# Decay differences in one operation per level, exponentials that carry signs and the key factor, and a new order in attention and gates

## The chip, the core and the metric

One core of a Trainium2 chip runs the whole program. The time is device microseconds of one execution. The kernel before takes 1636.86 us (median of three runs, 1635.97 to 1637.5).

## What is computed

Two transformer blocks over 512 tokens of width 1024, in fp32. The change lies in two mixers. One is the attention of block 1 (8 query heads, 2 groups of keys), whose keys are also compressed to one per 16 tokens:

```python
hp = rmsnorm(x, norm1_g) @ w_in                 # q, and keys and values of three branches
kc = rmsnorm(gelu(blocks(k0 + pe_k) @ wk1) @ wk2)   # compressed keys
vc = gelu(blocks(v0 + pe_v) @ wv1) @ wv2            # compressed values
q, k1, k2 = rmsnorm(q), rmsnorm(k1), rmsnorm(k2)    # per head of 64
o = g0*softmax(q kc^T) vc + g1*softmax(q k1^T, chosen blocks) v1 + g2*softmax(q k2^T, window) v2
```

The other is the gated recurrence of block 2 (4 heads of 128, two directions, the state first run over 256 context tokens):

```python
lf = logaddexp(log(lb), log1p(-lb) + log_sigmoid(z))   # log decay
k  = (1 - lb) * sigmoid(-z)
b  = cumsum(lf)
a[t, s] = sum_k q[t, k] * exp(b[t, k] - b[s, k]) * k[s, k]   # s <= t
o  = a @ v + (q * exp(b)) @ S
```

## The kernel before

**Products.** A product in fp32 is done as three matmuls on split halves (high and low part), by the helper `mm3` (L210 to L212). Weights come in by a DMA on SyncE's queue (`wload`, L222; two raw buffers), ScalarE makes the high part `wh` (L188 is its helper `act`), VectorE or GpSimd the low part `wl` (L191 is the helper `tt`; three buffers). PSUM has four banks for products ("mm"), one ("sm") and three ("aux").

**Who sets the order.** A scheduler puts the instructions of each engine into an order. It goes by the order in which the code emits them, and by priorities: weight loads are drawn ahead by `self.ahead` places. Every engine then works strictly through its own row, so an instruction that waits holds up all behind it.

**The gated recurrence** (`hgrn`, `hg_head`). `pj(h)` projects head h's gates: zf and zb (forward and backward; 512 tokens and 256 of context each) and the query q. `sig` turns them into `hgk` (key, one tile per direction), `hgkc` (key of the context) and `hgq`. Then `hg_head(h)` is emitted, and after it `pj(h+1)`, whose products are what TensorE has to do while a head's chain runs on the other engines. In `hg_head` ScalarE takes logarithms, giving log decays (`hgl`, and `hglc` for the context); VectorE scales the keys by 1−lb (`omlb`) and sums the logs by scans (L1450, L1452). The context's key goes through an exponential, a multiplication into `hgkc` and two transposes on TensorE (L1459) to the first state `hgS`. For the 512 tokens the matrix `a` is built in levels: blocks of 128 are cut in halves of 64, 32, 16 and 8. At each level `hgE` holds b minus a reference row for the later half, and the reference minus b for the earlier half: two subtractions of half width, the one on GpSimd, the other on VectorE. One exponential covers the four levels (128x2048). Later halves are multiplied by q, earlier ones by k. `hgek` and `hgeq` are the same for the innermost blocks. TensorE multiplies (L1515 for the innermost, L1525 and L1537 for the levels); `hgA` collects the results: a masked product, three plain copies per direction on VectorE (L1531) and eight copies under a mask (L1540). `hgke` and `hgqe` carry the state from block to block; its transposes come back through ScalarE as `hgkt`, and L1549, L1553 and L1554 form state and output.

**The attention** (`nsa_proj`). Eight projections of 128 columns in the order of the list `order`: the compressed branch's key and value (4, 5) first, then the keys 6 and 7, then q (0 to 3). Behind each of the six q and k tiles, squares are summed per head by a matmul (L859) into one bank with 12 rows. The compression (`compress`: 64 small matmuls, L971, a GELU, transposes, two small products, a norm with a power on GpSimd, `kcbd` and `vcz`) is a generator that is advanced once behind each projection but the first two. Behind the projections come the product for V (128x280), the start of the next product (ysH, `merge`), the norm factors broadcast by L879 (the tile `rb`), and `stack`, which splits q and k into halves (`qs`, `ks`) on ScalarE, VectorE and, for two of the q tiles, GpSimd. Then come the scores (L1061, L1063), the scores against compressed keys (L1019), and the transposes of the probabilities (L1083).

## Time and profile before

| | |
|---|---|
| median of three runs | 1636.86 us |
| the profiled execution | 1638.55 us |
| its span in the trace | 1636.8 us |
| mean granted clock of TensorE | 0.979 |
| TensorE busy | 1567.7 us, 96% |
| VectorE busy | 1130.2 us, 69% |
| ScalarE busy | 746.1 us, 46% |
| GpSimd busy | 418.0 us, 26% |

The times of rows and windows are counted from the start of the span. A granted clock of 1.00 in a window is the level of 2.4 GHz, 0.50 that of 1.2 GHz; values between are mixtures. "Idle before" is the time that an engine stood still ahead of an instruction, and the releaser is what ended it.

### The profile page before, as it was taken

The numbers are of one execution on the slowest core, as the hardware profiler recorded it, in microseconds if no ns is written. First come the engines' busy times: TensorE is split into PE (matmuls) and PEld (weight loads), VectorE is DVE, ScalarE is ACT, GpSimd is POOL, SyncE is SP. The second block draws the span as 40 slices with busy tenths as digits, with TensorE's granted clock in tenths as the row PEclk, the third lists the DMA queues.
The fourth block names the chain that finished last, engine by engine and source line by source line (L and its number), as shares of the span: only waits on it lengthen the run. The fifth ranks groups of instructions, "written<-read, shape, count | busy, mean of one in ns | idle before, by whom it ended". The sixth has DMA issues, their size and how long they took to land.

```text
span 1636.8 us, 22811 instructions
## 1 busy us (share of the span) xinstructions
PE 1567.7 (96%) x8573; PEld 1302.8 (80%) x8573; DVE 1130.2 (69%) x2141; ACT 746.1 (46%) x1301; POOL 418.0 (26%) x377
## 2 busy tenths in 40 slices
PE   7799998999999999999999999989989999999997
PEld 5678876677898888888887888878879888888886
DVE  8886626776679744763528788576877798676745
ACT  4364427553444213352335555556554664333432
POOL 1010204213000000000112222315320697555553
PEclk9899997999999999999999999999999999999999
DMA  5222510003356753832211011111211232323222
GB/s 179 75 81 64 158 47 26 20 21 117 104 192 217 243 198 130 262 109 90 84 64 65 27 39 52 60 52 52 65 65 57 91 103 91 103 90 103 91 87 81
DMA packets 58734, 157.85 MB, mean 96 GB/s; under 512 B 11904, under 2 KB 18816, under 8 KB 58496
## 3 DMA queue, kind: packets, MB, share of 16 engines
q1 hardware_dynamic: 58624, 156.40, 29.4%
q8 instruction: 67, 1.10, 0.3%
q14 instruction: 43, 0.35, 0.1%
HBM read 152.57 MB, written 2.10 MB: 94 GB/s over the span
## 4 chain that ended last, share of the span: by engine, by line
PE 79%; DVE 13%; ACT 5%; issue 2%; POOL 1%; DMA 0%; SPq 0%; DVEq 0%; ACTq 0%
PE ps_mm L210 22%; PE ps_mm L211 22%; PE ps_mm L212 22%; PE ps_sm L1094 2%; DVE wl L191 2%; PE ps_mm L1083 1%; DVE caccm L200 1%; ACT L188 1%; DVE hgE L191 1%; PE ps_sm L761 1%; ACT wh L188 1%; PE ps_aux L1537 1%; DVE caccf L200 1%; PE ps_mm L971 0%; PE ps_aux L1061 0%
## 5 line engine op out<-in xcount | busy, mean ns | idle before, releaser
L188 ACT ACTIVATE wh<-raw 128x1024 fp32r<-128x1024 f32 (+3 forms) x234 | 236.8, 1013 | 514.0 <-PE ps_mm L211 406.5
L191 DVE TENSOR_TENSOR wl<-raw,wh 128x1024 fp32r<-128x1024 f32 (+2 forms) x162 | 198.2, 1224 | 114.9 <-ACT wh L188 107.9
L200 DVE SCALAR_TENSOR_TENSOR caccf<-ps_mm,cwf,caccf 128x441 f32<-128x441 f32 (+2 forms) x278 | 188.5, 695 | 30.9 <-ACT ctapf L188 24.7
L191 POOL TENSOR_TENSOR wl<-raw,wh 128x1024 fp32r<-128x1024 f32 (+2 forms) x72 | 160.2, 2225 | 166.8 <-ACT wh L188 166.8
L212 PE MATMUL ps_mm<-h4H,wl 128*128 128x512 f32 (+1 forms) x352 | 131.2, 375 | 0.0
L211 PE MATMUL ps_mm<-h4L,wh 128*128 128x512 f32 (+1 forms) x352 | 131.1, 375 | 0.0
L210 PE MATMUL ps_mm<-h4H,wh 128*128 128x512 f32 (+1 forms) x352 | 129.7, 377 | 0.6 <-DVE caccf L200 0.4
L191 POOL TENSOR_TENSOR rr<-rv,nhalf 128x2 f32<-128x2 f32 x9 | 8.6, 957 | 431.9 <-DVE rv L197 431.9
L210 PE MATMUL ps_mm<-h2H,wh 128*128 128x512 f32 (+1 forms) x280 | 103.8, 372 | 0.0
L212 PE MATMUL ps_mm<-h2H,wl 128*128 128x512 f32 (+1 forms) x280 | 103.6, 371 | 0.0
L211 PE MATMUL ps_mm<-h2L,wh 128*128 128x512 f32 (+1 forms) x280 | 103.6, 371 | 0.0
L210 PE MATMUL ps_mm<-aH,wh 128*128 128x512 f32 (+1 forms) x272 | 102.6, 377 | 0.5 <-DVE x L191 0.5
L212 PE MATMUL ps_mm<-aH,wl 128*128 128x512 f32 (+1 forms) x272 | 102.7, 378 | 0.0
L211 PE MATMUL ps_mm<-aL,wh 128*128 128x512 f32 (+1 forms) x272 | 102.4, 377 | 0.0
L210 PE MATMUL ps_mm<-hH,wh 128*128 128x512 f32 x224 | 89.5, 406 | 10.0 <-ACT hH L188 9.0
L1229 DVE CUSTOM_DVE_ANT_0 msc<-wmod,cB,cols 128x1024 bf16<-128x1024 f32 x64 | 81.9, 1280 | 21.0 <-DMA wmod<-in_wmod 20.8
L211 PE MATMUL ps_mm<-hL,wh 128*128 128x512 f32 x224 | 89.7, 401 | 0.0
L212 PE MATMUL ps_mm<-hH,wl 128*128 128x512 f32 x224 | 89.5, 400 | 0.0
L211 PEld LDWEIGHTS ps_mm<-h4L,wh 128*128 128x128 f32 x352 | 66.2, 188 | 12.3 <-DVE h4L L200 0.4
L212 PEld LDWEIGHTS ps_mm<-h4H,wl 128*128 128x128 f32 x352 | 66.2, 188 | 12.2
L210 PEld LDWEIGHTS ps_mm<-h4H,wh 128*128 128x128 f32 x352 | 65.0, 188 | 13.5 <-issue 0.8
L210 PE MATMUL ps_mm<-faH,wh 128*128 128x512 f32 (+1 forms) x194 | 72.3, 373 | 0.0
(544 smaller groups left out, 4081.3 us busy)
## 6 DMA issues: line engine op xcount, KB each, us to landing
raw<-in_wup SPq DMA_DIRECT2D x76, 512.0 KB, 3.5
wmod<-in_wmod SPq DMA_DIRECT2D x48, 512.0 KB, 4.4
raw<-in_wdn SPq DMA_DIRECT2D x32, 512.0 KB, 3.5
raw<-in_win SPq DMA_DIRECT2D x28, 512.0 KB, 3.4
raw<-in_wout SPq DMA_DIRECT2D x8, 512.0 KB, 3.4
raw<-in_wdn2a SPq DMA_DIRECT2D x8, 512.0 KB, 3.5
raw<-in_wdn2b SPq DMA_DIRECT2D x8, 512.0 KB, 3.4
raw<-in_wdn2c SPq DMA_DIRECT2D x8, 384.0 KB, 3.0
```

The costliest lines, as they stand in the source:

```text
L188: return self.nc.scalar.activation(o, i, f, **k)
L191: return (e or self.nc.vector).tensor_tensor(o, a, b, op)
L200: return self.nc.vector.scalar_tensor_tensor(o, a, s, b, op0, op1)
L210: mm(ps, wh, xh, start=start, stop=False)
L211: mm(ps, wh, xl, start=False, stop=False)
L212: mm(ps, wl, xh, start=False, stop=stop)
L761: nc.tensor.matmul(py[32 * pl:32 * pl + 32, 128 * st:128 * st + 128], w[:, q4.start + pl, st], x[:, pl, 0:128], start=i == 0, stop=i == 2, ...
L1083: nc.tensor.transpose(tp[:, 128 * b:128 * b + 128], P[g, i][:, 128 * b:128 * b + 128], self.ident)
L1094: nc.tensor.matmul(O[64 * g:64 * g + 64, 128 * i:128 * i + 128], self.V[:, b, c:c + 64], PT[g][:, 128 * b:128 * b + 128], start=br == 0 an ...
L1229: ins = nc.vector.tensor_tensor_reduce(sc, w, cB[:, c], 1.0, bm[:, m:m + 1], OP.mult, OP.add, acc)
L1537: nc.tensor.matmul(ps[:, j], EE[:, li, 128 * j:128 * j + 128], vw(EE[:, li])[:, j], start=True, stop=True)
```

## The change

**In the recurrence.** Each level's difference becomes one full-width subtraction on VectorE, b minus the reference. Its sign is put right in the exponentials: a level's later half is exponentiated with a bias, its earlier half with scale −1, so that the one 128x2048 exponential becomes eight of 128x256 per direction. The bias is the logarithm of 1−lb (`lnom`, two small instructions in `hg_consts`): the key's factor goes to the query side, in `hgeq`, `hgE` and `hgqe`, and the two scalings of `hgk` and `hgkc` go away. `hgke` is no longer subtracted on GpSimd: four exponentials of 128x128 take the block's last decay as bias. The three plain copies into `hgA` go from VectorE to ScalarE; the eight masked copies per direction become two. `pj` is split: `pj1(h+1)`, the zf projection, is emitted ahead of `hg_head(h)`, and `pj2`, the rest, behind it.

**In the attention.** The projections for the compressed branch (4, 5) come last instead of first, and the compression is emitted in one piece behind the loop with `rb` and `stack`, its tiles in "aux" banks. The sums of squares become two groups of three matmuls with 32 rows each, in column tiles of the array, and the transposes behind them are of 96 rows. `vcz` is padded, so that the product with the compressed values takes all 128 rows.

```diff
@@ -787,13 +787,13 @@
...
         e = nc.gpsimd
-        self.hsel = p.tile([128, 6, 12], F32, name="hsel")
+        self.hsel = p.tile([128, 32], F32, name="hsel")
         e.memset(self.hsel, 0.0)
+        for g in range(2):
+            e.memset(self.hsel[64 * g:64 * g + 64, g:g + 1], 1.0)
...
         self.hselT = p.tile([128, 6, 128], F32R, name="hselT")
-        for a in range(6):
-            for g in range(2):
-                e.memset(self.hsel[64 * g:64 * g + 64, a, 2 * a + g:2 * a + g + 1], 1.0)
         for q in range(2):
@@ -829,19 +829,18 @@
...
         self.qp = qp
-        ss = self.mmtile((12, T), "aux")
+        slot = (4, 5, 0, 1, 2, 3)
+        sqs, s12 = [], []
         data = {}
...
         cmp = self.compress(p, data)
-        order = (4, 5, 6, 7, 0, 1, 2, 3)
+        order = (6, 7, 0, 1, 2, 3, 4, 5)
...
             unit(order[i], ps)
-            if i > 1:
-                next(cmp)
@@ -854,19 +853,33 @@
...
             self.tt(qk[a], ps, self.rb, OP.mult)
-            sq = qp.tile([128, T], F32, name="sq", tag="sq", bufs=1)
+            sp, tag, bufs = ((qp, "sq", 1), (p, "P03", 2), (p, "P03", 2))[slot.index(a) % 3]
+            sq = sp.tile([128, T], F32, name="sq", tag=tag, bufs=bufs)
             self.act(sq, qk[a], AF.Square)
-            nc.tensor.matmul(ss, self.hsel[:, a], sq, start=a == 4, stop=a == 3)
+            sqs.append(sq)
+            if len(sqs) == 3:
+                ss = self.mmtile((128, T), "aux")
+                for i in range(3):
+                    nc.tensor.matmul(ss[32 * i:32 * i + 32], self.hsel, sqs[i], start=True, stop=True,
+                                     tile_position=(0, 32 * i))
+                sp, tag, bufs = (p, "P03", 2) if s12 else (qp, "s12", 1)
+                t = sp.tile([96, T], F32, name="s12", tag=tag, bufs=bufs)
+                self.act(t, ss[:96])
+                s12.append(t)
+                sqs.clear()
...
-        s12 = qp.tile([12, T], F32, name="s12", tag="s12", bufs=1)
-        self.act(s12, ss)
-        tp = self.mmtile((128, 48), "aux")
-        for i in range(4):
-            nc.tensor.transpose(tp[:, 12 * i:12 * i + 12], s12[:, 128 * i:128 * i + 128], self.ident[:12, :12])
-        r = self.rsqrt(qp, tp, 48, 64, "rn")
+        rr = [qp.tile([128, 4, 2, 6], F32, name="rn" + x) for x in "vrt"]
+        for h in range(2):
+            tp = self.mmtile((128, 4, 3, 32), "aux")
+            for i in range(4):
+                nc.tensor.transpose(tp[:, i], s12[h][:, 128 * i:128 * i + 128], self.ident[:96, :96])
+            self.ts(rr[0][:, :, h].rearrange("p i (s g) -> p i s g", g=2), tp[:, :, :, 0:2], 1.0 / 64, OP.mult, EPS, OP.add)
+        rr = [x.rearrange("p i h s -> p (i h s)") for x in rr]
+        self.root(rr[1], rr[0], rr[2])
+        r = rr[1]
         tq = self.mmtile((12, T), "aux")
@@ -876,9 +889,12 @@
...
             rb = self.mmtile((128, T), "aux")
-            nc.tensor.matmul(rb, self.hselT[:, a], r12, start=True, stop=True)
+            nc.tensor.matmul(rb, self.hselT[:, slot.index(a)], r12, start=True, stop=True)
             self.stt(qk[a], qk[a], self.col(gcols[a]), rb, OP.mult, OP.mult)
...
+        for _ in cmp:
+            pass
@@ -941,7 +950,7 @@
...
         self.kcbd = p.tile([128, 64], F32, name="kcbd")
-        self.vcz = p.tile([128, 128], F32, name="vcz")
+        self.vcz = p.tile([128, 2, 128], F32, name="vcz")
         nc.gpsimd.memset(self.vcz, 0.0)
@@ -961,7 +970,7 @@
...
-            hid = self.mmtile((64, 128), "mm")
+            hid = self.mmtile((64, 128), "aux")
@@ -975,13 +984,13 @@
...
-            tp = self.mmtile((128, 64), "mm")
+            tp = self.mmtile((128, 64), "aux")
...
-        kp = self.mmtile((64, 64), "mm")
+        kp = self.mmtile((64, 64), "aux")
@@ -993,12 +1002,12 @@
...
-        vp = self.mmtile((128, 64), "mm")
+        vp = self.mmtile((128, 64), "aux")
...
-            self.act(self.vcz[s, 64 * (b % 2):64 * (b % 2) + 64], vp[s])
-        tp = self.mmtile((128, 64), "mm")
+            self.act(self.vcz[s, b // 2, 64 * (b % 2):64 * (b % 2) + 64], vp[s])
+        tp = self.mmtile((128, 64), "aux")
@@ -1103,8 +1112,7 @@
...
                     PcT.append(t)
-            rows = slice(64 * (j % 2), 64 * (j % 2) + 64)
-            nc.tensor.matmul(O, self.vcz[rows], PcT[j // 2][rows], start=False, stop=True, skip_group_check=True)
+            nc.tensor.matmul(O, self.vcz[:, j % 2], PcT[j // 2], start=False, stop=True, skip_group_check=True)
             H = self.qp.tile([128, T], F32R, name=f"ynH{j}", tag=f"qk{j}", bufs=1)
@@ -1314,6 +1322,10 @@
...
+        self.lnom = p.tile([128, 8], F32, name="lnom")
+        self.ts(self.lnom, self.omlb, 1e-37, OP.max)
+        self.act(self.lnom, self.lnom, AF.Ln)
@@ -1369,9 +1381,12 @@
...
-        def pj(h):
+        def pj1(h):
             pc = self.mmtile()
             zf, _ = self.proj2(I["w2zf"][h], hs, cs, pc[:, 0:TC])
+            return pc, zf
+        def pj2(h, pc, zf):
             zb, _ = self.proj2(I["w2zb"][h], hs, cs, pc[:, TC:])
@@ -1391,11 +1406,12 @@
...
-        gates = sig(0, pj(0))
+        gates = sig(0, pj2(0, *pj1(0)))
         for h in range(4):
+            first = pj1(h + 1) if h < 3 else None
             self.hg_head(p, h, *gates)
             self.ahead = 600
-            nxt = pj(h + 1) if h < 3 else self.hg_gproj()
+            nxt = pj2(h + 1, *first) if h < 3 else self.hg_gproj()
             self.ahead = 150
@@ -1422,7 +1438,7 @@
...
         v = self.hgv
-        om, nom = self.omlb, self.nomlb
+        nom = self.nomlb
         lc = p.tile([128, 2 * TC], F32, name="hglc", tag="hglc", bufs=1)
@@ -1433,11 +1449,6 @@
...
             self.bact(lc[:, s], kc[:, s], AF.Ln, scale=nom[:, c:c + 1], bias=1.0)
-        for d in range(2):
-            c = 4 * d + h
-            s = slice(TC * d, TC * d + TC)
-            self.ts(kl[d], kl[d], om[:, c:c + 1], mul)
-            self.ts(kc[:, s], kc[:, s], om[:, c:c + 1], mul)
         O = self.mmtile((128, 512), "sm")
@@ -1471,38 +1482,37 @@
...
             lo, up = (0, 1) if d == 0 else (1, 0)
+            ln = self.lnom[:, 4 * d + h:4 * d + h + 1]
             for li, m in enumerate((64, 32, 16, 8)):
-                bv = b.rearrange("p (n u m) -> p n u m", u=2, m=m)
-                ev = EE[:, li].rearrange("p (n u m) -> p n u m", u=2, m=m)
-                r = bv[:, :, 0, m - 1:m] if d == 0 else bv[:, :, 1, 0:1]
-                rb = r.to_broadcast([128, 256 // m, m])
-                self.tt(ev[:, :, up], bv[:, :, up], rb, sub, nc.gpsimd)
-                self.tt(ev[:, :, lo], rb, bv[:, :, lo], sub, nc.vector)
+                b2 = b.rearrange("p (n m) -> p n m", m=2 * m)
+                e = m - 1 + d
+                self.tt(EE[:, li].rearrange("p (n m) -> p n m", m=2 * m), b2,
+                        b2[:, :, e:e + 1].to_broadcast([128, 256 // m, 2 * m]), sub)
             eq = p.tile([128, T], F32, name="hgeq", tag="hgeq", bufs=2)
...
             self.tt(ek.rearrange("p (n m) -> p n m", m=8), b8, rb, sub)
-            self.bact(eq, ek, AF.Exp)
+            self.bact(eq, ek, AF.Exp, bias=ln)
             self.bact(ek, ek, AF.Exp, scale=-1.0)
...
             self.tt(ek, ek, k, mul)
-            self.bact(EE, EE, AF.Exp)
             for li, m in enumerate((64, 32, 16, 8)):
...
                 ev = sv(EE[:, li])
+                self.bact(ev[:, :, up], ev[:, :, up], AF.Exp, bias=ln)
+                self.bact(ev[:, :, lo], ev[:, :, lo], AF.Exp, scale=-1.0)
                 self.tt(ev[:, :, up], ev[:, :, up], sv(q)[:, :, up], mul)
...
             ke = p.tile([128, T], F32, name="hgke", tag="hgqe", bufs=3)
-            self.tt(ke.rearrange("p (n m) -> p n m", m=128), b4[:, :, e0:e0 + 1].to_broadcast([128, 4, 128]), b4, sub,
-                    nc.gpsimd)
-            self.bact(ke, ke, AF.Exp)
+            for j in range(4):
+                self.bact(ke[:, 128 * j:128 * j + 128], b4[:, j], AF.Exp, scale=-1.0, bias=b4[:, j, e0:e0 + 1])
             self.tt(ke, ke, k, mul)
             qe = p.tile([128, T], F32, name="hgqe", tag="hgqe", bufs=3)
-            self.bact(qe, b, AF.Exp)
+            self.bact(qe, b, AF.Exp, bias=ln)
             e0 = 127 if d == 0 else 0
@@ -1527,8 +1537,7 @@
...
                     k0, q0 = 2 * m * g + m * lo, 2 * m * g + m * up
-                    cp = nc.vector.tensor_copy
-                    cp(A[k0:k0 + m, :, q0:q0 + m], ps[k0:k0 + m, :, c:c + m])
+                    self.act(A[k0:k0 + m, :, q0:q0 + m], ps[k0:k0 + m, :, c:c + m])
             for li, m in ((2, 16), (3, 8)):
@@ -1536,8 +1545,8 @@
...
                                      stop=True)
-                for j in range(4):
-                    nc.vector.copy_predicated(vw(A.rearrange("p a b -> p (a b)"))[:, j], self.hmask[d, m], ps[:, j])
+                nc.vector.copy_predicated(vw(A.rearrange("p a b -> p (a b)")),
+                                          self.hmask[d, m][:, None].to_broadcast([128, 4, n, m]), ps)
             order = list(range(4)) if d == 0 else list(range(3, -1, -1))
```

**Where the rows stand now.** VectorE, head 0, from the scans of the logs up to the product that the hgkc transposes wait for. Before:

```order
L1452 SCALAR_TENSOR_TENSOR hglc<-ones,hglc 128x256
L196 TENSOR_SCALAR hgk<-hgk,omlb 128x512
L1450 SCALAR_TENSOR_TENSOR hgl<-rst,hgl 128x512
L196 TENSOR_SCALAR hgkc<-hgkc,omlb 128x256
L1452 SCALAR_TENSOR_TENSOR hglc<-ones,hglc 128x256
L191 TENSOR_TENSOR hgE<-hgl 128x4x64
L191 TENSOR_TENSOR hgE<-hgl 128x8x32
L191 TENSOR_TENSOR hgE<-hgl 128x16x16
L191 TENSOR_TENSOR hgE<-hgl 128x32x8
L191 TENSOR_TENSOR hgek<-hgl 128x512
L191 TENSOR_TENSOR hgqe<-hgqe,hgq 128x512
L191 TENSOR_TENSOR hgkc<-hgkc,hglc 128x256
```

After:

```order
L1461 SCALAR_TENSOR_TENSOR hgl<-rst,hgl 128x512
L1463 SCALAR_TENSOR_TENSOR hglc<-ones,hglc 128x256
L1461 SCALAR_TENSOR_TENSOR hgl<-rst,hgl 128x512
L191 TENSOR_TENSOR hgE<-hgl 128x512
L1463 SCALAR_TENSOR_TENSOR hglc<-ones,hglc 128x256
L191 TENSOR_TENSOR hgE<-hgl 128x512 x3
L191 TENSOR_TENSOR hgek<-hgl 128x512
L191 TENSOR_TENSOR hgE<-hgl 128x512 x4
L191 TENSOR_TENSOR hgek<-hgl 128x512
L191 TENSOR_TENSOR hgke<-hgke,hgk 128x512
L191 TENSOR_TENSOR hgqe<-hgqe,hgq 128x512
L191 TENSOR_TENSOR hgkc<-hgkc,hglc 128x256
```

The scalings are gone, all eight full-width subtractions and both of hgek stand ahead of that product, where only the first direction's stood.

ScalarE, head 1, from the logs to the first transposed keys (hgkt). Before:

```order
L188 ACTIVATE hglc<-hgkc,nomlb 128x256 x2
L188 ACTIVATE hgl<-hgk,nomlb 128x512 x2
L188 ACT_TABLE_LOAD
L188 ACTIVATE hglc<-hglc 128x256 x2
L188 ACTIVATE hgebe<-hgl 128x4
L188 ACTIVATE hgkt<-ps_aux 128x384
L188 ACTIVATE hgqe<-hgl 128x512
L188 ACTIVATE hgke<-hgke 128x512
L188 ACTIVATE hgE<-hgE 128x2048
L188 ACTIVATE hgeq<-hgek 128x512
L188 ACTIVATE hgE<-hgE 128x2048
L188 ACTIVATE hgkt<-ps_aux 128x256
```

After:

```order
L188 ACTIVATE hgA<-ps_aux 32x4x32 x2
L188 ACT_TABLE_LOAD
L188 ACTIVATE hglc<-hglc 128x256 x2
L188 ACTIVATE hgebe<-hgl 128x4
L188 ACTIVATE hgke<-hgl 128x128 x4
L188 ACTIVATE hgE<-hgE,lnom 128x4x64
L188 ACTIVATE hgE<-hgE 128x4x64
L188 ACTIVATE hgE<-hgE,lnom 128x8x32
L188 ACTIVATE hgE<-hgE 128x8x32
L188 ACTIVATE hgE<-hgE,lnom 128x16x16
L188 ACTIVATE hgE<-hgE 128x16x16
L188 ACTIVATE hgkt<-ps_aux 128x384
```

The copies into hgA stand between the logs and the table load, and six of the eight pieces of a direction ahead of hgkt.

TensorE, attention, from the norm factors (L879; L892 after) to the scores. Before:

```order
L212 MATMUL ps_mm<-ysH,wl 128x512
L879 MATMUL ps_aux<-r_1806,hselT 128x512 x6
L1061 MATMUL ps_aux<-ks,qs 128x256 x3
L1063 MATMUL ps_aux<-ks,qs 128x256 x3
L1061 MATMUL ps_aux<-ks,qs 128x256
L1063 MATMUL ps_aux<-ks,qs 128x256
L1061 MATMUL ps_aux<-ks,qs 128x384
L1063 MATMUL ps_aux<-ks,qs 128x384
```

After, with L980 for the compression's small matmuls, L1011 for the transpose to kcbd and L1070 and L1072 for the scores:

```order
L892 MATMUL ps_aux<-r_1795,hselT 128x512 x2
L980 MATMUL ps_aux<-cw,cD_2174 64x128 x8
L980 MATMUL ps_aux<-cw,cD_2176 64x128 x8
L980 MATMUL ps_aux<-cw,cD_2206 64x128 x8
L988 MATMUL ps_aux<-ident,chs_2204 128x64
L980 MATMUL ps_aux<-cw,cD_2208 64x128 x8
L988 MATMUL ps_aux<-ident,chs_2236 128x64
L994 MATMUL ps_aux<-cmpw_2172,chT_2240 64x64
L1006 MATMUL ps_aux<-cmpw_2172,chT_2244 128x64
L1011 MATMUL ps_aux<-ident,kz 128x64
L1070 MATMUL ps_aux<-ks,qs 128x256
L1072 MATMUL ps_aux<-ks,qs 128x256
```

The whole compression now stands between the norm factors and the scores; before it stood in the projections.

On TensorE in head 0, 28 products of 512 columns stand between the context's products of 256 columns and the first hgkc transposes, where 6 stood, and 20 between these and the second transposes, where 32 stood.

## Rows read from the trace of the kernel before

**Rows 1.** Chain that ended last: shares of the span by engine.
```profile
PE 79%; DVE 13%; ACT 5%; issue 2%; POOL 1%; DMA 0%; SPq 0%; DVEq 0%; ACTq 0%
```

**Rows 2.** Windows: busy us (instructions) by engine, PEclk (granted), DMA share, GB/s.
```profile
240.00:280.00 40.00, 34.57 (x175) 28.34 (x173) 21.13 (x50) 25.15 (x54) 14.28 (x13) 0.75 0.12 33
...
880.00:920.00 40.00, 37.02 (x261) 33.10 (x261) 37.77 (x87) 25.63 (x38) 8.54 (x9) 0.93 0.13 41
```

**Rows 3.** TensorE in time: start, us, instruction, [idle before <-releaser]; the stops.
```profile
878.39 0.69 PE L1459 MATMUL ps_aux<-ident,hgkc 128*128 128x128 f32 x2 [3.75 <-DVE hgkc L191]
...
916.29 0.79 PE L1554 MATMUL ps_sm<-hgv,hgA 128*128 128x128 f32 x2 [2.83 <-DVE hgA L1540]
...
958.72 0.94 PE L1549 MATMUL ps_aux<-hgv,hgkt 128*128 128x128 f32 x6 [2.23 <-ACT hgkt L188]
...
999.81 0.44 PE L1459 MATMUL ps_aux<-ident,hgkc 128*128 128x128 f32 x2 [2.02 <-DVE hgA L1540]
```

**Rows 4.** Windows behind the stops; columns as in rows 2.
```profile
880.00:884.00 4.00, 4.00 (x16) 3.14 (x16) 4.00 (x12) 4.00 (x6) 0.00 (x0) 0.82 0.00 0
916.00:920.00 4.00, 3.71 (x17) 3.71 (x18) 4.00 (x13) 3.88 (x6) 0.00 (x0) 0.50 0.00 0
920.00:924.00 4.00, 4.00 (x18) 3.55 (x17) 4.00 (x12) 0.55 (x2) 0.00 (x0) 0.70 0.00 0
960.00:964.00 4.00, 4.00 (x17) 3.60 (x16) 4.00 (x10) 3.76 (x5) 0.00 (x0) 0.58 0.00 0
1000.00:1004.00 4.00, 4.00 (x15) 3.19 (x14) 4.00 (x15) 4.00 (x6) 0.00 (x0) 0.61 0.01 2
```

**Rows 5.** VectorE in time, head 0; columns as in rows 3.
```profile
872.80 3.15 DVE L191 TENSOR_TENSOR hgE<-hgl 128x256 f32<-128x256 f32 x4
...
877.93 0.41 DVE L191 TENSOR_TENSOR hgkc<-hgkc,hglc 128x256 f32<-128x256 f32 x1
878.26 1.42 DVE L191 TENSOR_TENSOR hgE<-hgl 128x256 f32<-128x256 f32 x4
...
889.46 1.27 DVE L191 TENSOR_TENSOR hgek<-hgek,hgk 128x512 f32<-128x512 f32 x2
```

**Rows 6.** GpSimd in time, head 0; columns as in rows 3.
```profile
872.30 3.38 POOL L191 TENSOR_TENSOR hgE<-hgl 128x256 f32<-128x256 f32 x4
```

**Rows 7.** ScalarE's forms, 860-1040 us: busy us, mean ns, idle before <-releasers.
```profile
L188 ACT ACTIVATE hgE<-hgE 128x2048 f32<-128x2048 f32 x8 | 15.3, 1908 | 10.5 <-DVE hgE L191 10.5
...
L188 ACT ACTIVATE hgke<-hgke 128x512 f32<-128x512 f32 x8 | 5.0, 623 | 4.9 <-POOL hgke L191 4.9
...
L188 ACT ACTIVATE hglc<-hglc 128x256 f32<-128x256 f32 x8 | 3.8, 504 | 6.6 <-DVE hglc L1452 6.6
...
L188 ACT ACTIVATE hgkt<-ps_aux 128x256 f32<-128x256 f32 x8 | 3.0, 371 | 4.6 <-PE ps_aux L1459 4.6
```

**Rows 8.** VectorE's forms, 860-1040 us; columns as in rows 7.
```profile
L1540 DVE COPY_PREDICATED hgA<-mk,ps_aux 128x64 f32<-128x64 int32 x64 | 9.9, 221 | 5.0 <-PE ps_aux L1537 4.7
...
L1531 DVE COPY hgA<-ps_aux 32x128 f32<-32x128 f32 x16 | 4.6, 285 | 0.2
L196 DVE TENSOR_SCALAR hgk<-hgk,omlb 128x512 f32<-128x512 f32 x8 | 4.4, 551 | 0.7 <-ACT hgl L188 0.7
...
L1531 DVE COPY hgA<-ps_aux 64x256 f32<-64x256 f32 x8 | 3.4, 422 | 2.3 <-PE ps_aux L1525 2.1
```

**Rows 9.** TensorE's forms, 185-285 us; columns as in rows 7.
```profile
L971 PE MATMUL ps_mm<-cw,cD 128*64 128x128 f32 x64 | 8.2, 287 | 0.0
...
L859 PE MATMUL ps_aux<-sq,hsel 128*12 128x512 f32 x12 | 6.2, 596 | 0.0
```

**Rows 10.** TensorE and GpSimd in time, attention; columns as in rows 3.
```profile
253.83 0.40 PE L210 MATMUL ps_mm<-ysH,wh 128*128 128x512 f32 x1
...
272.02 6.92 PE L1019 MATMUL ps_aux<-kcbd,qk 128*128 128x64 f32 x32
...
266.73 5.68 POOL L191 TENSOR_TENSOR qs<-qk,qs 64x512 fp32r<-64x512 f32 x4 [7.86 <-ACT qs L188]
```

More of the change, by code (lines that the diff above doesn't have):

```diff
@@ L922, in stack @@
             self.tt(L, t[r], H[r].bitcast(F32), OP.subtract, self.nc.gpsimd if a in (2,3) else None)
-    def rsqrt(self, p, ss, n, width, nm):
-        v, r, t = (p.tile([128, n], F32, name=nm + x) for x in "vrt")
-        self.ts(v, ss, 1.0 / width, OP.mult, EPS, OP.add)
-        self.root(r, v, t)
-        return r
     def root(self, r, v, t):
```

## The prediction

> **What bounds the kernel now.** I read the chain of work that ended last first: TensorE holds 79% of it, VectorE 13%, ScalarE 5% [rows 1]. A change off TensorE therefore pays only where TensorE stands still or runs at its lower clock. The table of 40 us windows shows where, inside the two regions that the diff touches: 240 to 280 us (attention; 34.57 us busy, clock 0.75) and the gated recurrence, of which 880 to 920 us is the worst window (37.02 us busy, clock 0.93) [rows 2]. TensorE's instructions in time then show four stops, one per head: 3.75 us for hgkc from VectorE (head 0), 2.83 us for hgA from VectorE (head 1), 2.23 us for hgkt from ScalarE (head 2), 2.02 us for hgA from VectorE (head 3) [rows 3]; together 10.8 us. Behind each stop the granted clock is lower for a while, at its 1.2 GHz level instead of 2.4. A window with busy time B and clock c did 2(1−c)B at the low level and lost half of that: 0.72 us behind the first stop; 1.86 + 1.20 behind the second; 1.68 and 1.56 behind the third and fourth [rows 4]; together 7.0 us. So **the four stops cost 10.8 + 7.0 = 17.8 us**, by head 4.5, 5.9, 3.9 and 3.6. That is all that the recurrence part of the change can win on TensorE, whose matmuls there it doesn't touch.
>
> **Recurrence: what the change removes, adds and moves.** Each of the four heads has two directions, so everything counts eight times.
>
> *VectorE and GpSimd.* Today a level's difference is two half-width subtractions, the one on GpSimd, the other on VectorE. The same four VectorE subtractions take 3.15 us (872.80) while GpSimd does its four, and 1.42 us (878.26) with GpSimd idle [rows 5, 6]. So the two slow each other, and the new form, four full-width subtractions on VectorE, is to be priced against the mean of these, 2.3 us, not against 1.42. A full-width one I estimate at 0.60 us, from the 1.42 us for four halves: twice the elements is at most 2.84 us for four, and starting costs paid once make it less. So 2.4 to 2.8, that is +0.1 to +0.5 us. Removed from VectorE: the scaling of hgk (0.55; that of hgkc goes as well, beyond the sum), three copies into hgA per direction (4.6/8 + 3.4/8 = 1.0), and most of eight masked copies, which become two: 9.9/8 = 1.24 us now, 0.62 to 0.84 after (half, if only starting costs go; two 0.42 us copies of the same width if not) [rows 8]. Sum −1.4 to −2.1 us of VectorE per direction, 11 to 17 us in all, and GpSimd's part in it goes to zero. The scans and the other subtractions beside GpSimd also get their undisturbed times.
>
> *ScalarE.* One exponential of 128x2048 (1.91 us) becomes eight of 128x256. Four of them have a pointer operand, like the hglc exponentials of that width, 0.50 us; four have none, and the nearest row is the copy hgkt of that width, 0.37 us [rows 7]. Consecutive ones overlap by up to 0.1 us, an estimate from the start times, so 2.8 to 3.5 us: +0.9 to +1.6. hgke (0.62) becomes four of 128x128 with a pointer, 0.3 to 0.4 each: +0.7 to +1.0. The three copies into hgA come over: about 0.7 to 1.0. Sum +2.3 to +3.6 us per direction, +18 to +29 us in all; I take +22. What hides it: ScalarE today idles 10.5 us ahead of the eight hgE exponentials (waiting for VectorE), 4.9 us ahead of hgke (waiting for GpSimd) and 6.6 us ahead of the hglc exponentials (VectorE's scan) [rows 7], 22.0 us in all, and these waits are for the work that gets shorter. hgke no longer waits for GpSimd at all. So ScalarE's line is full afterwards, not overfull. If the waits don't shrink, its own line grows by what it adds (the second rival).
>
> *Order.* On TensorE the next head's first projection (24 products of 256 columns and 24 of 512) moves ahead of the head. At head 0 there stand 28 products of 512 columns between the 256-column ones and the first hgkc transposes, where there were 6: 22 more, at 0.234 us from start to start, 5.1 us of filler. Before, TensorE ran dry at 874.6 (878.39 − 3.75 [rows 3]). After, it would run dry at 879.7. VectorE's product hgkc, awaited there, ends at 878.34 now (877.93 + 0.41 [rows 5]). Between VectorE's first scan and that product the new order has eight full-width subtractions (4.8), four scans (3.8), two hgek subtractions, hgke and hgqe (0.6 each, 2.4): 11.0 us from 865.6, so 876.6. **Stop 1 goes**, with its clock: −4.5. But only 20 products then stand between these transposes and the head's own matmuls, where 32 stood; the last VectorE operands there (the hgek products) I replay at 886.5 where they now end at 890.7 (889.46 + 1.27 [rows 5]), and TensorE is there at about 885: so some 1 us comes back, net −3.5. At head 1 the same replay has the masked copy end at 911.4 where TensorE now waits for it until 916.29, and TensorE's filler reach 913: **stop 2 goes**, −5.9. Heads 2 and 3 hang on ScalarE (hgkt stands behind hgE's exponentials, and the new order keeps six of the eight pieces ahead of it) and on a PSUM buffer that hgA's last masked copy frees. There I take a third of 7.5: −2.5. Sum **−12 us**, bounds −4 (head 0 alone) and −17.8 (all).
> Three hgA copies now stand between ScalarE's logarithms and the table load for the exponentials. The matmuls they wait for are issued some 2 us before that load, so I price the wait at nothing; uncovered it is up to 2 us a head.
>
> **Attention.** The compression (L971 twice, 8.2 us together [rows 9], and some 1 us of small matmuls) leaves the projection, where TensorE never waits, and goes behind the last rb product, where it waits for the stacking on ScalarE. So the projection ends 9 us earlier. The sums (L859, six matmuls in twelve records, 6.2 us [rows 9]) lose at most the 1 us of one matmul, since in the order only two of the six tiled ones are neighbours; the wider transposes behind them give 1 us back. Nothing net.
> The Trainium skill (TensorE: Matmul & The Clock Gate, "Measured speedup vs the span model") has three column tiles of this size run 2.38 times as fast; by it, an estimate, 6.2 us would become 2.6 and the total 3.6 us less. No row of this trace shows three such matmuls side by side, and the sum goes without it.
> Behind rb, compression fills time in which TensorE does little but waits for ScalarE: four low halves of the stack run on GpSimd from 266.73 to 272.41, and the block of L1019 matmuls starts at 272.02, 18.2 us behind the end of the V product at 253.83 [rows 10]. But the score matmuls, which today run inside that time, now stand behind the whole chain: hidden products, GELU, transposes, and a power on GpSimd that is queued behind those four GpSimd rows. I replay the chain: scores from 20.8 us behind the V product, L1019's successor done at 28.7 (full clock) to 34 (half) where L1019 is at 25.1 today (272.02 + 6.92), less the 9 us gained: −5.4 to −0.1 us, and the scatter of a replayed chain is 3 us. I take **−1**.
>
> **The sum.** 1638.55 us is the profiled execution; 1638.55 − 12 − 1 = 1625.5. The median of the runs shown is 1.7 below that execution, so **1624 us**. The forecast's own range is 1618 to 1630.
>
> **The rivals.**
> *All stops close and attention keeps its gain*: −17.8 − 4 = −21.8, so 1615 us. For it speaks that three of four stops wait for VectorE, which loses work everywhere. Against it: fewer products are left between the transposes and the head's own matmuls.
> *ScalarE takes VectorE's place*: stops 1 and 2 close, but hgkt and the hgek exponentials, behind sixteen pieces, come later, and new stops of 2 us (3 with the clock) appear in two or three heads: −12 + 8 = −4, so 1631 to 1633 us. For it: +18 to +29 us on ScalarE against 22.0 us of idle time. Against it: those waits are for what gets shorter.
> *Slower by the same line*: ScalarE absorbs nothing of its idle time, because its pieces still come one by one as VectorE delivers them. Then each head's last hgek exponential is up to 2 × 2.7 = 5.4 us later, and TensorE's filler (20 products, 4.7 us) is shorter than what it has to bridge. With half of that uncovered, 2.7 us a head, and 4 us from attention at half clock: +10.8 + 4 − 4.5 (stop 1 still goes) = +10, so 1647 us. It decides from the point where that exponential ends later than now, counted from the head's logarithms.
> *Nothing moves*: the stops shift from one operand to the next and cost the same: 1635 to 1638 us.
>
> **How the numbers follow.** Forecast 0.46; all closes 0.17; ScalarE in VectorE's place 0.20; nothing moves 0.09; slower 0.08. About 0.2%, 3.3 us, is what a measurement of this kernel tells from no change. Faster takes the first three less a little of the third, 0.82; same 0.10; slower 0.08. The range reaches from the all-closes case to the upper end of the ScalarE case: 1613 to 1634.
>
> **What would show it.** Right: no wait of TensorE over 1 us for hgkc or hgA at heads 0 and 1; clocks of 0.95 and more right behind them; VectorE's full-width hgE subtractions at 0.6 to 0.7 us each everywhere; no GpSimd row for hgE or hgke. Wrong: waits of TensorE for ScalarE's hgkt or hgA copies, or for hgek; a low clock from 245 to 280 us that lasts longer than now (it starts 9 us earlier); the block of L1019's successor starting later than 272 us.

## The result

The changed kernel takes **1610.84 us** (median of four runs, 1609.62 to 1614.30) against 1637.18 us before: a ratio of 0.9844, 95% interval 0.9830 to 0.9857. On another chip it took 1613.72 us against 1636.10, a ratio of 0.9857 (0.9842 to 0.9871). So it is 22 to 26 us faster. The forecast had the sign, but said 13 us; the measured time is 2.2 us below the low end of its range (1613 us), and on the other chip 0.7 us above it.

The chain that ended last in the profiled execution of the changed kernel (span 1608.1 us) against [rows 1]:

```profile
PE 81%; DVE 11%; ACT 3%; issue 2%; POOL 2%; DMA 1%; SPq 0%; DVEq 0%; ACTq 0%; POOLq 0%
```

Windows of 40 us, columns as in [rows 2]. What happens in the recurrence at 880 to 920 us happened some 7 us later before:

```profile
240.00:280.00 40.00, 33.48 (x209) 28.38 (x209) 27.38 (x58) 28.72 (x72) 17.49 (x18) 0.91 0.16 47
...
880.00:920.00 40.00, 39.80 (x317) 35.80 (x316) 31.16 (x59) 28.21 (x64) 0.00 (x0) 1.00 0.17 54
```

All that TensorE waits for in the recurrence, 840 to 1020 us (line, releaser: us in total, times, longest), where [rows 3] had 10.8 us:

```profile
PE ps_sm L1562 <- ACT hgS L188: 1.2, 1, 1.2
PE ps_aux L1558 <- ACT hgkt L188: 0.9, 2, 0.6
PE ps_sm L1563 <- DVE hgA L1548: 0.2, 1, 0.2
```

No stop for hgkc or hgA is left, and no low clock: 1.00 in every window of 4 us from 824 to 1016 us. By windows of 4 us, idle time and clock cost 11.4 + 7.7 = 19.0 us in the recurrence before (832 to 1044 us) and 2.3 + 0 after. The clock's part differs between executions: e1_attn below, whose rows there are before's, has 11.4 + 4.2.

VectorE's forms there, as in [rows 8]. Its busy time in the recurrence fell from 147.6 us (860 to 1045) to 124.0 us (850 to 1018):

```profile
L191 DVE TENSOR_TENSOR hgE<-hgl 128x512 f32<-128x512 f32 x32 | 19.9, 680 | 0.0
...
L1548 DVE COPY_PREDICATED hgA<-mk,ps_aux 128x256 f32<-128x256 int32 x16 | 7.0, 437 | 11.7 <-PE ps_aux L1546 9.8 <-issue 1.9
```

ScalarE's, as in [rows 7]; its busy time rose from 99.4 to 119.6 us in the same stretches:

```profile
L188 ACT ACTIVATE hgE<-hgE,lnom 128x256 f32<-128x256 f32 x32 | 15.9, 497 | 0.0
...
L188 ACT ACTIVATE hgE<-hgE 128x256 f32<-128x256 f32 x32 | 12.9, 405 | 0.0
L188 ACT ACTIVATE hgke<-hgl 128x128 f32<-128x128 f32 x32 | 10.2, 389 | 2.5 <-PE ps_sm L1562 2.5
```

**Where the time went.** I set the same instruction of both traces side by side and took the distance between such marks: the first L761 matmul, the first ysH product, the first h2H product (second half of block 1), the first product cH of 256 columns (the gates), the last product with hgA, and the first h4H product (second half of block 2). In us, of the profiled execution of each kernel:

| kernel | start | S5 | attention | to the gates | recurrence | second mixer | last two of these |
|---|---|---|---|---|---|---|---|
| before | 66.2 | 102.6 | 275.3 | 396.0 | 205.1 | 211.5 | 416.7 |
| after | 64.0 | 102.5 | 270.8 | 395.9 | 184.5 | 210.0 | 394.5 |
| e13_after | 64.9 | 102.6 | 271.5 | 395.9 | 184.5 | 210.0 | 394.6 |
| e1_attn | 66.2 | 102.6 | 271.3 | 395.9 | 202.0 | 211.6 | 413.6 |
| e2_rec | 66.1 | 102.6 | 275.4 | 396.0 | 184.5 | 210.1 | 394.6 |
| e3_nosplit | 64.4 | 102.6 | 271.4 | 395.9 | 184.5 | 211.7 | 396.2 |
| e4_split | 65.3 | 102.6 | 276.7 | 396.0 | 204.2 | 210.4 | 414.6 |
| e5_gphalf | 65.5 | 102.6 | 270.6 | 397.5 | 192.8 | 210.2 | 403.0 |
| e6_copies | 64.2 | 102.6 | 270.9 | 395.9 | 187.8 | 211.7 | 399.5 |
| e7_oneexp | 63.9 | 102.6 | 271.4 | 395.9 | 192.4 | 211.1 | 403.5 |
| e8_dveonly | 65.9 | 102.6 | 275.3 | 395.9 | 198.3 | 211.6 | 409.9 |
| e9_keyscale | 65.6 | 102.6 | 271.6 | 396.0 | 186.4 | 212.5 | 399.0 |
| e10_cpdve | 64.9 | 102.6 | 271.6 | 395.9 | 187.7 | 211.8 | 399.5 |
| e12_qslow | 64.2 | 102.5 | 271.5 | 395.9 | 184.6 | 211.7 | 396.3 |

Of the 28.7 us between the two spans, 22.1 lie in the last column, 4.5 in the attention and 2.2 in the start. The last column is best read as one: with fewer stops in the recurrence TensorE does other products behind it, not in it. It scatters too: before and e1_attn, whose rows there are the same on all engines, differ by 3.1 us in it, and before's is the longer. So a difference of 2 or 3 us in this column is no proof by itself. The start is in part scatter: one and the same kernel has 64.0 and 64.9 there. Whether any of the 2.2 us belongs to the change, the runs don't settle.

### The profile page after: what moved, and what is told of

The parts are those of the page before. It is cut to its first block, busy times and chain, and to the rows that moved or that the text cites. A ratio compares the mean times of both kernels' runs of the same rounds, so it can differ in the third digit from the quotient of the medians.

```text
span 1608.1 us, 22768 instructions
## 1 busy us (share of the span) xinstructions
PE 1547.3 (96%) x8577; PEld 1291.8 (80%) x8577; DVE 1106.0 (69%) x2055; ACT 770.1 (48%) x1409; POOL 382.5 (24%) x327
## 4 chain that ended last, share of the span: by engine, by line
PE 81%; DVE 11%; ACT 3%; issue 2%; POOL 2%; DMA 1%; SPq 0%; DVEq 0%; ACTq 0%; POOLq 0%
PE ps_mm L210 23%; PE ps_mm L212 22%; PE ps_mm L211 22%; PE ps_sm L1103 2%; DVE caccm L200 2%; PE ps_mm L1092 1%; DVE wl L191 1%; PE ps_aux L1546 1%; PE ps_sm L761 1%; ACT L188 1%; ACT wh L188 1%; DVE caccf L200 1%; PE ps_aux L1535 1%; PE ps_aux L1070 1%; PE ps_sm L1562 0%
## 5 line engine op out<-in xcount | busy, mean ns | idle before, releaser
L210 PE MATMUL ps_mm<-aH,wh 128*128 128x512 f32 (+1 forms) x272 | 102.6, 377 | 0.5 <-DVE x L191 0.5
L211 PEld LDWEIGHTS ps_mm<-h4L,wh 128*128 128x128 f32 x352 | 66.2, 188 | 12.5 <-DVE h4L L200 0.4
L212 PEld LDWEIGHTS ps_mm<-h4H,wl 128*128 128x128 f32 x352 | 66.2, 188 | 12.2
```

Of the source, the lines that this page charges most:

```text
L210: mm(ps, wh, xh, start=start, stop=False)
L211: mm(ps, wh, xl, start=False, stop=False)
L212: mm(ps, wl, xh, start=False, stop=stop)
```

## The parts apart, and together

Theory: the relief of VectorE closes the stops. Rival: the projection that is emitted first does it. Also asked: whether attention and recurrence add up.

**e1_attn**: before with the attention alone, that is the diff down to the product with the padded `vcz`, for instance

```diff
-        order = (4, 5, 6, 7, 0, 1, 2, 3)
+        order = (6, 7, 0, 1, 2, 3, 4, 5)
...
+        for _ in cmp:
+            pass
```

> Before with the attention part of the change alone (order of the projections, compression behind rb, tiled sums, padded vcz). By the marks in the two traces the attention gives 4 to 5 us (the first L1083 transposes 7.8 us earlier, the last ysH product 5.9 us earlier, of which 2.2 us stood already at the start of the span): 1631 to 1633 us, and the first mark, the first product at 9.03 us, stays where it was if those 2.2 us are scatter of one execution. Rival, that the attention's gain is given back later: within 1.5 us of before, 1636 to 1638 us.

Measured: 1633.14 us, ratio 0.9979 (0.9969 to 0.9989): −3.2 us by the medians, and 4.0 in the attention by the marks. The gain is there and stays.

**e2_rec**: before with the recurrence alone, that is the diff from `lnom` on.

> Before with the recurrence part alone, split projection included. If the parts add, 16.7 us of stops and low clock inside the recurrence and some 4.5 us behind it (the norm and the second mixer): minus 20 to 22, 1615 to 1617 us. Rival, that what is gained behind the recurrence comes from the new time of all that stands ahead of it (attention moved): only the stops, minus 15 to 17, 1620 to 1622 us.

Measured: 1616.25 us, ratio 0.9882 (0.9867 to 0.9897): −20.1 us, with the same 394.6 us in the last column as after. The gain behind the recurrence is not attention's.

**e3_nosplit**: after with the projection in one piece again:

```diff
-            first = pj1(h + 1) if h < 3 else None
             self.hg_head(p, h, *gates)
...
-            nxt = pj2(h + 1, *first) if h < 3 else self.hg_gproj()
+            nxt = pj(h + 1) if h < 3 else self.hg_gproj()
```

> After without the split projection: the whole of the next head's projection is emitted behind the head, as before. Theory that the relieved VectorE closes the stops by itself: within 3 us of after, 1610 to 1614 us. Rival, that the filler moved ahead closes them: the stop for hgkc at head 0 comes back with its low clock (VectorE's product at about 870 us in after's time, TensorE dry some 5 us sooner), and smaller ones at heads 1 to 3: 1616 to 1622 us.

Measured: 1613.48 us, ratio 0.9863 (0.9848 to 0.9877). More than the time, the rows tell: set side by side without line numbers, the instructions of this kernel and of after stand in the same order on all five engines. The 28 products ahead of the first hgkc transposes, which the prediction put down to the split, stand there without it.

**e4_split**: before with the split alone, the lines above the other way round.

> Before with the split projection alone. Theory that the relieved VectorE closes the stops: the filler only moves them to the head's own matmuls, minus 0 to minus 4: 1633 to 1637 us. Rival, that the order does it: minus 8 to minus 16: 1621 to 1629 us.

Measured: 1637.79 us, ratio 1.0008 (0.9998 to 1.0018). No gain. All four stops are there (3.73, 2.98, 2.93 and 2.00 us), and head 0's hgkc transposes stand behind 6 products as before, though other rows of TensorE in the recurrence have moved. The split gains nothing, in either company. In e1, without any edit of the recurrence, the rows there are before's; so the other edits of the recurrence made the scheduler move the filler. Which of them did it, no run separates.

## What of the recurrence it is

Theory G: GpSimd beside VectorE was the main cost. Theory W: VectorE's own removed work was.

**e5_gphalf**: after, with differences by halves on two engines:

```diff
-                self.tt(EE[:, li].rearrange("p (n m) -> p n m", m=2 * m), b2,
-                        b2[:, :, e:e + 1].to_broadcast([128, 256 // m, 2 * m]), sub)
+                self.tt(ev[:, :, up], bv[:, :, up], rb, sub, nc.gpsimd)
+                self.tt(ev[:, :, lo], bv[:, :, lo], rb, sub, nc.vector)
```

> After with each level's difference made by halves again, the later half on GpSimd and the earlier on VectorE, both as b minus the reference; exponentials, copies and the rest as in after. Theory G, that GpSimd beside VectorE was the main cost: VectorE's halves cost 0.8 us instead of 0.36, its scans and other subtractions are slowed again, and the later halves come last; over half of the recurrence's 20 us is lost: 1621 to 1628 us, with stops for hgkc or hgA back. Theory W, that VectorE's removed scalings and copies were the main share: at most 4 us lost, 1611 to 1617 us.

Measured: 1620.99 us, ratio 0.9908 (0.9892 to 0.9924). The last column is 8.4 us longer than after's, and the column to the gates 1.6 us. TensorE's waits, 828 to 1028 us:

```profile
PE ps_sm L1565 <- DVE hgA L1550: 5.9, 4, 2.6
PE ps_aux L1470 <- DVE hgkc L191: 1.0, 1, 1.0
```

The stops for hgA are back, in four places. **e8_dveonly** is the other direction, before with nothing but the engine of these subtractions changed:

```diff
-                self.tt(ev[:, :, up], bv[:, :, up], rb, sub, nc.gpsimd)
+                self.tt(ev[:, :, up], bv[:, :, up], rb, sub, nc.vector)
```

> Before with nothing changed but the engine of GpSimd's subtractions in the recurrence: all eight halves of a direction and that of hgke on VectorE. VectorE gets five more instructions a direction, 4 x 0.36 + 0.6 = 2.0 us, and loses the slowing by GpSimd (1.7 us on the halves, 0.3 to 0.8 each on scans, hglc and hgek). Theory G: the stops shrink, 6 to 12 us faster, 1624 to 1630 us. Theory W: VectorE's line is no shorter and nothing is gained or some is lost: 1635 to 1642 us.

Measured: 1629.41 us, ratio 0.9958 (0.9943 to 0.9973), 6.2 us faster, 6.8 by the last column: GpSimd's work is given to VectorE on top of its own, and the kernel gets faster. VectorE in time, head 0 (columns as in [rows 5]):

```profile
867.04 0.68 DVE L1452 TENSOR_TENSOR_SCAN hglc<-ones,hglc 128x256 f32<-128x256 f32 x1
...
870.00 2.75 DVE L191 TENSOR_TENSOR hgE<-hgl 128x256 f32<-128x256 f32 x8
...
873.87 0.42 DVE L191 TENSOR_TENSOR hgkc<-hgkc,hglc 128x256 f32<-128x256 f32 x1
```

All eight halves take 2.75 us, less than four did in the first of [rows 5], and hgkc is ready at 874.3 instead of 878.3. The remaining waits of TensorE, 832 to 1036 us:

```profile
PE ps_aux L1537 <- DVE hgA L191: 4.6, 2, 3.7
PE ps_aux L1544 <- DVE hgA L1531: 2.4, 1, 2.4
PE ps_aux L1549 <- ACT hgkt L188: 1.1, 2, 0.7
```

They are at heads 0 and 1 but for 0.7 us. **The stops of heads 2 and 3 are gone with GpSimd's part alone**, the one for ScalarE's hgkt too. For that one e8 alone is no proof of the relief: the scheduler has also put this hgkt (949.26) ahead of ScalarE's exponential of hgE (954.27), behind which it stood before (958.20 behind 955.34). The trace of after settles it, as told under heads 2 and 3 below.

**e6_copies** and **e10_cpdve**: after with the copies on VectorE again, in e6 with the masked ones apart as well:

```diff
-                    self.act(A[k0:k0 + m, :, q0:q0 + m], ps[k0:k0 + m, :, c:c + m])
+                    cp = nc.vector.tensor_copy
+                    cp(A[k0:k0 + m, :, q0:q0 + m], ps[k0:k0 + m, :, c:c + m])
```

> After with the copies into hgA on VectorE again and eight masked copies per direction: VectorE gets back 1.4 to 1.6 us per direction, 11 to 13 us in all, ScalarE loses 6 to 8 us. Theory G: VectorE has slack now, 0 to 3 us slower: 1611 to 1615 us. Theory W: 5 to 10 us slower, stops for hgA back at heads 1 and 3: 1616 to 1622 us.

> After with the plain copies into hgA on VectorE, the masked copies merged as in after. The order of the second mixer's rows on TensorE and VectorE is then that of before, row by row. Theory O, that 4 to 5 us of the gain lie in that order and not in the recurrence: the recurrence has no stop over 1.5 us, and behind it the waits of before come back (3.0 us for wl, 1.7 for mW, 1.8 for yml): 3 to 5 us slower than after on the same chip. Rival, that these waits went because the recurrence ends sooner: within 1.5 us of after.

Measured: e6 1615.05 us, ratio 0.9870 (0.9854 to 0.9887); e10 1617.93 us against 1613.72 of after on the same chip, ratio to before 0.9881 (0.9866 to 0.9896). Both have 399.5 us in the last column: merging the masked copies is worth nothing that shows, the plain copies 4.9 us. But no stop over 1.4 us comes back in the recurrence (idle 2.98 us, 824 to 1016, against 2.33 in e13). By idle time and clock, 4.7 us lie in the second mixer and 0.7 in the recurrence (the table puts 3.2 into the recurrence, because other products stand in it). The second mixer's rows on TensorE and VectorE, one by one, stand in before's order in e10 and in after's in e13. TensorE's waits there in e10 (1020 to 1232 us), and below in e13 (1016 to 1228 us):

```profile
PE ps_aux L211 <- DVE wl L191: 3.0, 1, 3.0
PE ps_aux L1967 <- DVE mW L200: 2.7, 3, 1.7
PE ps_aux L1967 <- DVE yml L200: 2.6, 2, 1.8
```

```profile
PE ps_aux L1966 <- DVE yml L200: 1.4, 2, 0.7
...
PE ps_aux L211 <- DVE wl L191: 1.1, 1, 1.1
...
PE ps_aux L1966 <- DVE mW L200: 0.9, 1, 0.9
```

Idle time and clock behind the recurrence (212 us from 1016): 13.3 + 2.6 in e10, 9.5 + 1.6 in e13; before had 13.1 + 2.7 from 1044, with the same waits (1044 to 1256 us):

```profile
PE ps_aux L211 <- DVE wl L191: 3.0, 1, 3.0
PE ps_aux L1957 <- DVE mW L200: 2.7, 3, 1.6
PE ps_aux L1957 <- DVE yml L200: 2.5, 2, 1.8
```

Before, e1, e4, e6, e8 and e10, whose rows on TensorE and VectorE there have before's order, have these waits of 3.0 us for wl (2.98 in e4); after, e2, e3, e12 and e13, in after's order, 1.1 to 1.2. e5, in after's order but for a few rows on TensorE, has 2.7 there and 1.0 to 1.1 where before's order has 1.7. So 3 to 5 us of the gain (3 where the low clock of the last section comes in) go with an order that the scheduler made of code that the change doesn't touch. That the order alone makes them is not shown: no kernel here changes it and nothing else, and e5, with after's order on VectorE, still waits 2.7 us for wl.

**e7_oneexp**: after with the key's factor and the sign as before, all on VectorE, and one exponential of 128x2048. **e9_keyscale**: of this only the factor.

```diff
+            self.ts(kl[d], kl[d], self.omlb[:, c:c + 1], mul)
+            self.ts(kc[:, s], kc[:, s], self.omlb[:, c:c + 1], mul)
...
-                self.bact(ev[:, :, up], ev[:, :, up], AF.Exp, bias=ln)
+                self.bact(ev[:, :, up], ev[:, :, up], AF.Exp)
```

> After with sign and key factor as before: the two scalings per direction on VectorE, signed half-width subtractions (all eight per direction on VectorE, none on GpSimd), one exponential of 128x2048, no bias; hgke, copies, attention as in after. VectorE gets 1.0 us for the scalings and about 0.4 for the halves per direction, ScalarE loses 0.9 to 1.6. If the pieces help by feeding VectorE and TensorE earlier, 4 to 8 us slower, 1615 to 1620 us. If they are only a cost that ScalarE's idle time hides, within 3 us of after: 1609 to 1614 us.

> After with the key factor back on VectorE (the two scalings per direction, no bias in the exponentials); the eight pieces, full-width differences and copies stay. Theory P, that the previous run's loss came from the one long exponential holding up what stands behind it on ScalarE: the pieces remain, so the recurrence loses at most 3 us to after: 1611 to 1617 us with its own row order of the second mixer. Theory S, that the scalings on VectorE cost it: 6 us and more inside the recurrence, 1618 to 1623 us.

Measured: e7 1624.40 us (1619.21 to 1625.42), ratio 0.9920 (0.9899 to 0.9940), last column 8.9 us longer than after's, slower than either expectation; e9 1614.83 us against 1613.72 on the same chip, ratio to before 0.9863 (0.9846 to 0.9879), last column 4.4 longer. By the marks the factor on VectorE costs 4.4 us, of which 1.9 in the recurrence, and the long exponential with its half-width differences another 4.5. This split of the 8.9 is rough: the marks are of e9's slowest execution and of e7's and e13's fastest. By the medians e9 loses only 1.1 us to after, and by the ratios e7 loses 10 to 12. What the long exponential does shows in e7's waits, 828 to 1028 us:

```profile
PE ps_aux L1552 <- DVE hgA L191: 2.6, 2, 1.7
PE ps_aux L1559 <- ACT hgA L188: 1.7, 1, 1.7
```

TensorE now waits for ScalarE's copies into hgA, which it nowhere does in after, and for the PSUM buffer that VectorE's masked product frees.

**Counted up**, by the last column: halves on GpSimd 8.4, copies 4.9, factor and sign 8.9, split 0, together 22.2 of the 22.1 us. That this closes to 0.1 us is chance: the column scatters by up to 3 us, and hgke's move off GpSimd is in none of the parts. What holds is that neither G nor W does it alone. GpSimd's part is 6 to 8 us from either side (e8, e5), under half; the rest is spread over the copies, the factor and the exponentials in pieces.

**e12_qslow**: after, with `self.nc.gpsimd if a == 2` instead of `if a in (2,3)` in `stack`, to shorten GpSimd's row ahead of the compressed keys.

> After with the low halves of the last q tile on VectorE, so that two instead of four of them stand ahead of the power on GpSimd in the attention. If GpSimd's row holds up the scores (2.44 us ahead of L1011), that stop shrinks by 1 to 1.5 us: 1 to 2 us faster than after on the same chip. If ScalarE's stack holds them up anyway, within 0.5 us.

> After itself, on the same chip as the three others, so that differences of a few us can be read: 1610 to 1614 us. Its first marks (first product at 8.4 us) differ from before's by the scatter of the start, which is no part of the change.

Measured: e12 1612.39 us, e13 1613.72 us; the stop ahead of L1011 is 1.40 us in both, so the 1.3 us between the medians are not this stop's. In e12 GpSimd comes free at 257.8, but the sum that its power waits for is there only at 261.0. (In the profiled execution of after, with 2.44 us, it was the other way round: the sum was there at 259.0, and GpSimd came free at 259.9.) VectorE's four low halves, nearly all of the time beside a busy GpSimd, take 6.76 us, 1.7 each, where one with GpSimd idle took 0.69 before: VectorE is slower beside GpSimd here too.

## Why the prediction fell short

Two terms of the recurrence's −12 us failed: heads 2 and 3, priced at −2.5, and the second mixer behind it, priced at nothing. The recurrence part alone brought −20.1 (e2). All four signs of being right came true, but none of them bore on these two terms.

- **Cost of the stops.** 17.8 us, measured 19.0 with the smaller gaps. It held for that execution. **That this was all that the recurrence part could win did not:** idle time and clock fell by 4.5 us in the second mixer (from 13.1 + 2.7 to 9.5 + 1.7), which the sum had at nothing because the change doesn't touch its code. The scheduler reordered it (e10).
- **VectorE.** Full-width subtractions are spaced by 0.60 us (0.68 each with overlap) as estimated, the masked copies 0.87 us per direction against a bound of 0.84. But 147.6 − 124.0 = 23.6 us fell away where the sum had 11 to 17. What it priced was right: subtractions +0.7, scaling of hgk −4.4, copies −8.0 and masked copies −2.9 are −14.6 us. The rest is the scaling of hgkc, 3.8 us, which it left beyond the sum, and some 6 us of instructions that only got faster: the scan of hglc from 0.92 to 0.68 us, hgek from 0.95 to 0.68, hgkc from 0.62 to 0.42 (eight each). The prediction named them and gave them no number. Before, 860 to 1045 us:

```profile
L191 DVE TENSOR_TENSOR hgek<-hgl 128x512 f32<-128x512 f32 x8 | 7.5, 953 | 0.0
L1452 DVE TENSOR_TENSOR_SCAN hglc<-ones,hglc 128x256 f32<-128x256 f32 x8 | 7.4, 924 | 0.0
...
L196 DVE TENSOR_SCALAR hgkc<-hgkc,omlb 128x256 f32<-128x256 f32 x8 | 3.8, 473 | 0.1
```

- **ScalarE.** +22 us taken, +20.2 measured; the pieces 0.497 and 0.405 us. Its waits shrank as argued, and the two rivals that set it as the new bound didn't come.
- **Order.** The printed rows were right, their cause wrong (e3, e4).
- **Heads 0 and 1.** Counted from the same mark, hgkc is ready at 876.7 in before's time (predicted 876.6 and its own 0.4), the hgek products at 886.6 (886.5), so the replay row by row held to 0.3 us. At head 1 nothing waits. At head 0 1.24 us of waiting come back (1 predicted), but that this fits is luck, for no matmul waits for hgek. TensorE waits for ScalarE's hgS (879.32 to 879.58), behind a high half wh that had waited 2.61 us for its weights' DMA:

```profile
879.63 0.49 PE L1562 MATMUL ps_sm<-hgS,hgqe 128*128 128x128 f32 x2 [1.24 <-ACT hgS L188]
...
878.36 1.06 ACT L188 ACTIVATE wh<-raw 128x1024 fp32r<-128x1024 f32 x1 [2.61 <-DMA raw<-in_w2hq]
```

- **Heads 2 and 3: the step that failed.** It read the releaser in [rows 3], ScalarE's hgkt, as the cause at head 2, and took a third of 7.5 us because hgkt keeps standing behind hgE's exponentials. ScalarE was itself waiting for VectorE there, 4.58 us for a scan and 2.14 us for hgE. Before:

```profile
952.69 0.51 ACT L188 ACTIVATE hglc<-hglc 128x256 f32<-128x256 f32 x1 [4.58 <-DVE hglc L1452]
955.34 1.91 ACT L188 ACTIVATE hgE<-hgE 128x2048 f32<-128x2048 f32 x1 [2.14 <-DVE hgE L191]
...
958.20 0.47 ACT L188 ACTIVATE hgkt<-ps_aux 128x384 f32<-128x384 f32 x1
```

  After, hgkt still stands behind six pieces, but ScalarE no longer waits between the logs and it. It ends 9.2 us behind the start of the logs, where it took 14.9, and TensorE needs it only 0.9 us later:

```profile
936.98 0.49 ACT L188 ACTIVATE hgkt<-ps_aux 128x384 f32<-128x384 f32 x1
...
938.39 0.38 PE L1558 MATMUL ps_aux<-hgv,hgkt 128*128 128x128 f32 x2
```

  That GpSimd slowed VectorE there shows in e8: the scan of hglc takes 0.68 us instead of 0.91 to 1.11, the scaling of hgk 0.46 instead of 0.48 to 0.80. Head 3 waited for VectorE's masked copy, and that stop is gone too. Both stops went; with the one small wait of 0.64 us that is left counted against them, 6.9 of the 7.5 us. With −6.9 for −2.5 the sum for the recurrence is −16.4; measured, by idle time and clock, −16.7.
- **Attention.** The V product ends 12.6 us earlier, 10.4 without the start (9 predicted), the first scores come 20.3 us behind it (20.8), L1028 ends after 29.3 (28.7 to 34), its clock 0.57 in the window from 264 to 268 us and 1.00 in the next:

```profile
241.25 0.40 PE L210 MATMUL ps_mm<-ysH,wh 128*128 128x512 f32 x1
...
266.42 4.17 PE L1028 MATMUL ps_aux<-kcbd,qk 128*128 128x64 f32 x32
...
286.88 0.49 PE L1092 MATMUL ps_mm<-ident,P 128*128 128x128 f32 x2 [3.65 <-DVE P L196]
```

  The block takes 4.17 us, 6.92 in [rows 10]. A new wait of 3.65 us for VectorE's scaling gives part back. −4.5 by the marks, −3.2 by the medians of e1, −1 predicted: of the bounds −5.4 and −0.1 it took the wrong end, without a row for the choice. The tiled sums took 5.2 us after 6.2 [rows 9], the 1 us of the one adjacent pair. The Trainium skill's factor for three column tiles (TensorE: Matmul & The Clock Gate, "Measured speedup vs the span model") was not put to the test: in no run here do three of them stand side by side.
- **The rivals.** "All stops close" at 1615 us was the one whose mechanism came true; it had 0.17. It too had nothing for the second mixer.
- **What is left.** With 4.4 us more at heads 2 and 3, 4.5 in the second mixer and 2.2 in the attention the forecast would have been 1613 us. The measured 1610.84, and 1613.72 on the other chip, lie within 2.2 us of that, which is scatter of the size seen above.

## What to carry to other kernels

Follow a stop's releaser one step further before giving it a price: the engine named may itself be waiting. Where two engines work in the same stretch, take the duration that an instruction has while the other is idle as the price of relief, and count it for every instruction there, not only for those that are edited. And where a scheduler sets the order, run a variant with each edit alone before saying which edit moved a row, and look at the order of code that isn't touched.

## What was not expected of the hardware

With after's order of rows in the recurrence and the second mixer, two of five profiled executions (e3 and e12, but not after, e2 and e13) show a stretch at 1.2 GHz in which TensorE never stood still. e12, windows of 4 us, columns as in [rows 2]:

```profile
1080.00:1084.00 4.00, 4.00 (x25) 3.31 (x24) 1.45 (x3) 2.29 (x5) 1.35 (x2) 0.98 0.00 0
1084.00:1088.00 4.00, 4.00 (x12) 3.20 (x11) 1.73 (x2) 4.00 (x13) 2.44 (x3) 0.60 0.29 78
```

The same windows of e13, whose rows there are the same:

```profile
1080.00:1084.00 4.00, 4.00 (x26) 3.38 (x25) 0.59 (x1) 1.43 (x3) 0.49 (x1) 1.00 0.00 0
1084.00:1088.00 4.00, 4.00 (x20) 3.27 (x19) 2.60 (x4) 4.00 (x12) 3.30 (x4) 1.00 0.07 10
```

It costs 1.7 us (4.00 × 0.40 and the 0.08 before it), which is the whole difference of e3 and e12 to after, e2 and e13 in the last column. The last stop ahead of it, 1.1 us, lies over 20 us back. What sets it off stays open; for differences under 2 us between two such kernels it is reason enough to compare several executions.
